# Operands of a seven-product matmul made between plain FFN blocks, with three banks, other groups and longer-lived weight pools

## The chip, the cores and the metric

The kernel runs on one core of one Trainium2 chip. The metric is the device time of one execution in microseconds. A core has a matrix engine (TensorE, PE in the profile, with PEld for its weight loads), VectorE (DVE), ScalarE (ACT), GpSimd (POOL) and SyncE (SP), which here issues nearly all DMAs. On-chip data lies in SBUF; matmuls write to eight PSUM banks.

## What is computed

One step of a one-layer decoder for 512 prompt tokens and 8 x 8 sample tokens, which share all weights: 576 tokens of 1024 channels in float32. Two SwiGLU FFNs enclose a token-mixing part (an RWKV-7 scan, a causal convolution, cross-attention into 256 memory tokens, three gates):

```python
def _swiglu(x, w_up, w_down):
    hg = x @ w_up
    return (jax.nn.silu(hg[..., :D_FF]) * hg[..., D_FF:]) @ w_down

x = x + 0.5 * _swiglu(_rmsnorm(x, p['ffn1_norm']), p['ffn1_w_up'], p['ffn1_w_down'])
m, wkv, shift, conv = _token_mixing(_rmsnorm(x, p['mix_norm']), ...)
x = x + m
x = x + 0.5 * _swiglu(_rmsnorm(x, p['ffn2_norm']), p['ffn2_w_up'], p['ffn2_w_down'])
```

D_FF is 2816. The change is in both FFNs and in the pools that the whole kernel takes its weights from.

## The kernel before

Activations lie with channels on partitions: x is eight tiles of 128 channels x 576 tokens (N), treated as two halves of 288 (H). Precision is kept by splitting each float32 operand into a high and a low part (`split`: ScalarE casts the high part, VectorE subtracts it from the source for the low one), and multiplying three times: high by high, high by low, low by high (`mm3k`, line 94, and line 353).

An FFN (`ffn`) has 22 blocks of 128 hidden channels. A block needs two up-projections (gate and value), a Silu, a product (`hidden`, line 421), and a split into one of the rooms listed in `ROOMS`.

- Blocks 0 to 4 are plain (`plain`): two products of 48 matmuls each over x scaled by the norm weight, then a multiplication by the tokens' 1/rms (line 410). A weight tile of 128 x 1024 is loaded (`wload`, line 70) and split in two halves of 512 columns, each a pair of tiles.
- Blocks 5 to 21 are Strassen blocks (`strassen`): the two up-projections together form a 2 x 2 product of block matrices (gate and value by two token halves, with the 1024 channels in even and odd groups), made from seven products of 12 matmuls, 84 in all where a plain block has 96. Four of the seven weight sides are sums, made by GpSimd (`total`, line 344); four of the token sides are differences. All seven are split. The results are combined by VectorE from three banks (lines 363 to 373).
- The token sides come from `operands`: for each of four pairs of channel tiles, the scaled x and four differences, one of them on GpSimd (line 319), and seven splits. It is written after the five plain blocks and before the first Strassen block. Its scaled x uses the same tiles (t1, t2) as the blocks, its differences the tiles m1 and p.
- Down-projections go by groups of blocks, `FGROUPS` = (4, 4, 4, 4, 2, 4): when a group's hidden tiles are there, its eight down products (`down`, one for each 128 output channels; evicted at line 417) are written behind the blocks of the next group, evenly. The last group's come at the end with the sums of squares of the next norm.

The weight tiles come from two pools, opened anew for each stage: `wp` for raw weights (3 tiles in the FFNs, 2 in the mixing) and `wq` for split pairs (5 and 3). Tile pools hand a buffer on when its last reader is done. The order of instructions on each engine is set when the kernel is built, by a planner that takes the source order as priority, models times, and lets ready work go ahead of work that waits; on the chip each engine's queue and SP's queue run in that order.

At the end of FFN1 the memory tokens are projected to keys and values (`mem_load`, `mem_k`, `mem_v`) around the last norm row, and `mix_norm` makes the mixing stage's operands. The mixing stage's first weights are the `win` tiles; `merge`, between the mixing and FFN2, starts with `wya` weights and four tiles yl (lines 1021 to 1029).

Of the kernel before, what the change touches and what calls it, by code (L numbers as in the profile page):

```python
# [22 lines left out]
FGROUPS = (4, 4, 4, 4, 2, 4)  # L23
PLAIN = 5

ROOMS = (8, 9, 10, 11, 12, 0, 1, 2, 3, 4, 5, 6, 8, 9, 10, 11, 0, 1, 8, 9, 10, 11)
# [23 lines left out]
class _Builder:  # L50
# [16 lines left out]
    def wload(self, src, n, pool=None, tag="", cap=512):  # L67

        w = self.wp.tile([128, 1024], F32, name="w")[:, :n]
        self.dma(w if len(src.shape) == 2 else w.rearrange("p (j c) -> p j c", j=src.shape[1]), src)  # L70
        parts = []
        for c in range(0, n, cap):
            x = w[:, c:min(c + cap, n)]
            hl = [(pool or self.wq).tile([128, cap], F32R, name="w" + t + tag)[:, :x.shape[1]] for t in "hl"]
            self.split(hl[0], hl[1], x)
            parts.append(hl)
        return lambda i, a, b: parts[a // cap][i][:, a % cap:(b - 1) % cap + 1]
# [74 lines left out]
    def build(self):  # L152
        tc, a = self.tc, self.a
        with ExitStack() as st:
            E = st.enter_context
            cp = E(tc.tile_pool(name="cp", bufs=1))
            self.xp = E(tc.tile_pool(name="xp", bufs=1))
# [14 lines left out]
            with ExitStack() as sf:  # L172
                F = sf.enter_context
                self.psum(F, p=8)
                self.wp, self.wq = (F(tc.tile_pool(name=t, bufs=b)) for t, b in (("wp", 3), ("wq", 5)))
# [3 lines left out]
                self.strassen_pools(F)  # L179
                x = [x1p.tile([128, N], F32, name=f"x{k}") for k in range(8)]  # L180
                self.dma(self.pv, a["pv"])
                raw = []
                for n in (2, 2, 2):
                    w = self.wp.tile([128, 1024], F32, name="w")
                    raw += [w[:, 384 * k:384 * (k + 1)] for k in range(n)]
                raw += [self.sp.tile([128, 512], F32, name="p")[:, :384] for _ in range(2)]
# [24 lines left out]
            self.wp, self.wq = (s_ps.enter_context(tc.tile_pool(name=t, bufs=b)) for t, b in (("wp", 2), ("wq", 3)))  # L211
# [36 lines left out]
            self.wp, self.wq = (E(tc.tile_pool(name=t, bufs=b)) for t, b in (("wp", 3), ("wq", 5)))  # L248
# [17 lines left out]
    def strassen_pools(self, F):  # L266

        self.xe = F(self.tc.tile_pool(name="xe", bufs=1))
        self.sp = F(self.tc.tile_pool(name="sp", bufs=3))
# [13 lines left out]
    def rows(self, fp, t, h):  # L283

        r = fp.tile([128, H], F32, name="r" + str(h), bufs=1)
# [12 lines left out]
    def operands(self, x, fp, g, r):  # L298

        V, G = self.V, self.G  # L300
        out = []
        for p in range(4):
            t = []
            for k in (2 * p, 2 * p + 1):
                t.append(fp.tile([128, N], F32, name=f"t{k % 2 + 1}"))
                for h, ri in enumerate(r):
                    c = slice(h * H, (h + 1) * H)
                    V.scalar_tensor_tensor(t[-1][:, c], x[k][:, c], self.par(g, k), ri, ALU.mult, ALU.mult)
            b11, b12, b21, b22 = (u[:, h * H:(h + 1) * H] for u in t for h in range(2))
            t1, t2 = (self.sp.tile([128, 512], F32, name="p")[:, :H] for _ in range(2))  # L310
            t3, t4 = (fp.tile([128, H], F32, name="m1") for _ in range(2))
            ops = {}

            def part(n, src):
                o = ops[n] = self.xe.tile([128, 2, H], F32R, name=n + str(p))
                self.split(o[:, 0], o[:, 1], src)

            part("b11", b11)
            G.tensor_tensor(t3, b12, b22, ALU.subtract)  # L319
            V.tensor_tensor(t1, b11, b12, ALU.subtract)  # L320
            V.tensor_tensor(t2, b22, t1, ALU.add)
            part("t2", t2)
            V.tensor_tensor(t4, b21, t2, ALU.subtract)
            part("b21", b21)
            part("t1", t1)
            part("t4", t4)
            part("b22", b22)
            part("t3", t3)
            out.append(ops)
        return out  # L330

    def strassen(self, fp, wu, i, xs):
# [3 lines left out]
        w = []  # L336
        for m in range(2):
            w.append(self.wp.tile([128, 1024], F32, name="w"))
            self.dma(w[m], wu[i + m])
        a11, a12, a21, a22 = (t.rearrange("p (k e c) -> p k e c", e=2, c=128)[:, :, e, :] for t in w for e in range(2))  # L340
        def total(u, v):
            s = self.sp.tile([128, 512], F32, name="p")
            s = s.rearrange("p (k c) -> p k c", c=128)
            G.tensor_tensor(s, u, v, ALU.add)  # L344
            return s
        def product(p, src, b, first):
            hl = [self.wq.tile([128, 512], F32R, name="w" + t) for t in "hl"]
            v = [t.rearrange("p (k c) -> p k c", c=128) for t in hl]
            self.split(v[0], v[1], src)
            for k in range(4):  # L350
                c = slice(128 * k, 128 * k + 128)
                for q, (l, o) in enumerate(((0, 0), (0, 1), (1, 0))):
                    self.T.matmul(p, hl[l][:, c], xs[k][b][:, o], start=first and k == 0 and q == 0,  # L353
                                  stop=k == 3 and q == 2, skip_group_check=True)
        pa, pb, pc = (self.bank()[:, :H] for _ in range(3))
        m1 = fp.tile([128, H], F32, name="m1")
        t1, t2 = (fp.tile([128, N], F32, name=n) for n in ("t1", "t2"))
        product(pa, a11, "b11", True)
        A.copy(m1, pa)
        p1 = total(a21, a22)  # L360
        p2 = total(p1, a11)
        product(pb, p2, "t2", True)
        V.tensor_tensor(t1[:, H:], pb, m1, ALU.subtract)  # L363
        product(pa, a12, "b21", False)
# [811 lines left out]
```

## Time and profile before

| quantity | value |
|---|---|
| time, median of 3 runs | 1564.11 us (1562.04 to 1569.45) |
| profiled execution, own time | 1566.99 us |
| its span, first to last instruction | 1564.5 us |
| mean granted TensorE clock | 0.962 |
| DMA moved | 144.64 MB, mean 92 GB/s |
| VectorE, ScalarE, GpSimd busy | 64%, 43%, 13% of the span |

The profile shows one execution. Busy time of an engine is the time in which it had at least one instruction under way; overlapping instructions count once. The row of 40 slices gives tenths of each slice of 39 us. The table of stretches gives busy time and counts for chosen windows, and so shows which stage an average hides. The chain of work that ended last is followed back from the end: each piece is a start, a length, and an engine with the tile it wrote.

### The profile page before, as it was taken

How to read it: one execution, taken by the hardware profiler on the slowest of the kernel's cores; microseconds unless marked ns; L12 is line 12 of the kernel's file. 1: busy time of each engine (PE TensorE's matmuls, PEld its weight loads, DVE VectorE, ACT ScalarE, POOL GpSimd, SP SyncE). 2: the span in 40 equal slices, each digit the busy share in tenths (PEclk: the TensorE clock that was granted, in tenths of full speed). 3: DMA queues.
4: the chain of work that ended last, by engine and by line, in shares of the span. 5: the costliest groups of instructions: out<-in, count | busy, mean ns of one | idle time of the engine just before them, and what ended most of it. 6: DMA issues, size and time to landing. Idle time of an engine off the chain costs nothing.

```text
span 1564.5 us, 27277 instructions
## 1 busy us (share of the span) xinstructions
PE 1475.8 (94%) x10786; PEld 1389.8 (89%) x10786; DVE 1000.1 (64%) x1993; ACT 673.3 (43%) x1397; POOL 197.4 (13%) x165
## 2 busy tenths in 40 slices
PE   8959999999989999999999999979996999999987
PEld 8959999998989889878879878769996899999987
DVE  5586676666775559769456455356447666667666
ACT  5343443433456645444446443334333344334342
POOL 0033222222100000000000000000002322231320
PEclk9979999999989999999899999989998899999998
DMA  5212223323543143223213124175211223323222
GB/s 185 75 34 88 82 83 102 100 68 94 157 121 108 42 146 87 58 75 102 64 52 112 42 79 121 53 240 173 93 55 34 81 82 96 108 82 95 78 85 68
DMA packets 97626, 144.64 MB, mean 92 GB/s; under 512 B 43916, under 2 KB 55564, under 8 KB 97500
## 3 DMA queue, kind: packets, MB, share of 16 engines
q1 hardware_dynamic: 96924, 142.33, 29.8%
q8 instruction: 84, 1.38, 0.4%
q10 hardware_dynamic: 576, 0.59, 0.1%
q14 instruction: 42, 0.34, 0.1%
HBM read 126.36 MB, written 16.53 MB: 91 GB/s over the span
## 4 chain that ended last, share of the span: by engine, by line
PE 81%; DVE 10%; DMA 3%; ACT 3%; POOL 2%; issue 1%; SPq 0%; DVEq 0%; POOLq 0%; ACTq 0%
PE p L94 46%; PE p L353 20%; DVE wl L81 2%; PE g L829 1%; DVE t L81 1%; PE c L947 1%; DMA w<-wu 1%; POOL p L344 1%; PE c L951 1%; PE c L944 1%; DVE pr L906 1%; DVE x L417 1%; ACT wh L80 1%; POOL m L319 1%; DMA w<-win 1%
## 5 line engine op out<-in xcount | busy, mean ns | idle before, releaser
L94 PE MATMUL p<-x,wh 128*128 128x288 f32 (+1 forms) x3232 | 679.7, 302 | 13.2 <-ACT wh L80 13.0
L94 PEld LDWEIGHTS p<-x,wh 128*128 128x128 f32 (+1 forms) x3232 | 526.9, 190 | 27.2 <-issue 15.2
L94 PE MATMUL p<-x,wl 128*128 128x288 f32 (+1 forms) x1616 | 485.5, 301 | 1.5 <-DVE wl L81 1.5
L80 ACT CAST wh<-w 128x512 fp32r<-128x512 f32 (+2 forms) x359 | 213.6, 598 | 275.4 <-PE p L94 134.8
L81 DVE TENSOR_TENSOR wl<-w,wh 128x512 fp32r<-128x512 f32 (+2 forms) x359 | 243.1, 679 | 130.8 <-ACT wh L80 121.7
L94 PEld LDWEIGHTS p<-x,wl 128*128 128x128 f32 (+1 forms) x1616 | 306.3, 190 | 7.3 <-issue 3.3
L353 PE MATMUL p<-t,wh 128*128 128x288 f32 x1088 | 224.0, 300 | 19.5 <-ACT wh L80 9.6
L353 PEld LDWEIGHTS p<-t,wh 128*128 128x128 f32 x1088 | 176.2, 191 | 23.9 <-DVE t L363 11.9
L353 PE MATMUL p<-b,wh 128*128 128x288 f32 x816 | 170.6, 301 | 26.2 <-ACT b L80 17.9
L81 DVE TENSOR_TENSOR wl<-p,wh 128x512 fp32r<-128x512 f32 (+1 forms) x138 | 120.0, 874 | 106.5 <-ACT wh L80 105.3
L80 ACT CAST wh<-p 128x512 fp32r<-128x512 f32 (+1 forms) x138 | 82.8, 617 | 193.7 <-POOL p L344 155.9
L353 PE MATMUL p<-t,wl 128*128 128x288 f32 x544 | 161.5, 297 | 0.1
L353 PEld LDWEIGHTS p<-b,wh 128*128 128x128 f32 x816 | 132.7, 191 | 30.1 <-ACT b L80 19.0
L344 POOL TENSOR_TENSOR p<-w 128x512 f32<-128x512 f32 x68 | 88.8, 1306 | 265.7 <-DMA w<-wu 250.8
L353 PE MATMUL p<-b,wl 128*128 128x288 f32 x408 | 121.3, 297 | 0.0
L319 POOL TENSOR_TENSOR m<-t,t 128x288 f32<-128x288 f32 x8 | 13.9, 1731 | 809.1 <-PE p L94 701.0
L344 POOL TENSOR_TENSOR p<-p,w 128x512 f32<-128x512 f32 x68 | 91.7, 1348 | 160.8 <-DVE wl L81 157.4
L353 PEld LDWEIGHTS p<-t,wl 128*128 128x128 f32 x544 | 103.3, 190 | 0.8 <-DVE wl L81 0.8
L353 PEld LDWEIGHTS p<-b,wl 128*128 128x128 f32 x408 | 78.1, 191 | 0.0
L417 DVE SCALAR_TENSOR_TENSOR x<-p,x 128x288 f32<-128x288 f32 x160 | 68.0, 449 | 6.9 <-PE p L94 6.6
L80 ACT CAST x<-t 128x576 fp32r<-128x576 f32 (+1 forms) x60 | 36.4, 610 | 49.4 <-DVE t L421 45.2
L971 DVE SCALAR_TENSOR_TENSOR st<-c,gc,mg 64x64 f32<-64x64 f32 x56 | 15.9, 283 | 58.7 <-PE c L962 58.0
(317 smaller groups left out, 2049.1 us busy)
## 6 DMA issues: line engine op xcount, KB each, us to landing
w<-wu SPq DMA_DIRECT2D x85, 512.0 KB
w<-win SPq DMA_DIRECT2D x44, 512.0 KB
w<-wd SPq DMA_DIRECT2D x80, 256.0 KB
d_mb<-gate SPq DMA_DIRECT2D x16, 288.0 KB
w<-wo SPq DMA_DIRECT2D x8, 512.0 KB
x<-x SPq DMA_DIRECT2D x8, 288.0 KB
d_x<-x SPq DMA_DIRECT2D x16, 144.0 KB
d_g<-gate SPq DMA_DIRECT2D x8, 288.0 KB
```

The lines of the kernel that those rows point to most:

```text
L80: self.A.copy(hi, x)
L81: self.V.tensor_tensor(lo, x, hi.bitcast(F32), ALU.subtract)
L94: self.T.matmul(p, l, x[r][:, c], start=k == 0 and i == 0, stop=k == n - 1 and i == 2)
L319: G.tensor_tensor(t3, b12, b22, ALU.subtract)
L344: G.tensor_tensor(s, u, v, ALU.add)
L353: self.T.matmul(p, hl[l][:, c], xs[k][b][:, o], start=first and k == 0 and q == 0, stop=k == 3 and q == 2, skip_group_check=True)
L417: V.scalar_tensor_tensor(x[m][:, c], p, 0.5, x[m][:, c], ALU.mult, ALU.add)
L829: T.matmul(ps[:, i * 128:(i + 1) * 128], kb[o, c + i].rearrange("p a t -> p (a t)"), ra[o, c + i].rearrange("p a t -> p (a t)"), start=Tru ...
L906: V.tensor_tensor(pr, tt[:, :n, :e].unsqueeze(2).broadcast_to([np_, n, m, e]), l3[:, t:e, :e].unsqueeze(1).broadcast_to([np_, n, m, e]), A ...
L944: T.matmul(ps[64:, 64 * h:64 * h + 64], gr[:64, h, c, 64:], vu[:64, c, 64 * h:64 * h + 64], start=h == 0 or not inter, stop=not inter)
L947: T.matmul(ps[64:, :128], l, r, start=False, stop=i == len(inter) - 1)
L971: V.scalar_tensor_tensor(mn[s, s], ps[s, 256 + 64 * h:320 + 64 * h], gc[s, c:c + 1], mg[s, s], ALU.mult, ALU.add)
```

## The change

In words:

- `operands` makes one set for one pair of channel tiles and is called after plain blocks 1, 2, 3 and 4. The scaled x lies in a tile of its own, n (one buffer), 1/rms in one 576-wide tile rn; differences and splits are done on wide tiles where two lie side by side; all differences are on VectorE.
- `strassen` starts with the product of the sum p2, keeps three banks with two other products between two uses of one, and ends with a22. t2's sign handling changes with the order, the number of VectorE operations doesn't.
- The raw weights of a block are asked for one block ahead (`raws`).
- `FGROUPS` is (6, 4, 4, 4, 4); `ROOMS` follows it.
- Pools wp (2) and wq (3) are opened once for the whole kernel; the FFNs add two raw tiles (we) and one pair (wf), and hand tiles out in turn. So the FFNs have four raw tiles and four pairs, the mixing two and three as before.
- FFN1's first raw weights, the last group's down weights and the memory tokens are split into other tiles of xe. `mem_v` is made in two halves, with the norm row between them.

```diff
-FGROUPS = (4, 4, 4, 4, 2, 4)
+FGROUPS = (6, 4, 4, 4, 4)
+NORMED = 1
-ROOMS = (8, 9, 10, 11, 12, 0, 1, 2, 3, 4, 5, 6, 8, 9, 10, 11, 0, 1, 8, 9, 10, 11)
+ROOMS = (8, 9, 10, 11, 12, 0, 1, 2, 3, 4, 8, 9, 10, 11, 5, 6, 7, 0, 8, 9, 10, 11)
...
+    def weight_pools(self, E=None, raw=0, split=0):
+        self.wps, self.wqs, self.nw, self.nq = [self.wp] * 2, [self.wq] * 3, 0, 0
+        if E:
+            self.wps += [E(self.tc.tile_pool(name="we", bufs=raw))] * raw
+            self.wqs += [E(self.tc.tile_pool(name="wf", bufs=split))] * split
+    def wtile(self):
+        self.nw += 1
+        return self.wps[self.nw % len(self.wps)].tile([128, 1024], F32, name="w")
+    def wparts(self):
+        self.nq += 1
+        return [self.wqs[self.nq % len(self.wqs)].tile([128, 512], F32R, name="w" + t) for t in "hl"]
...
-        self.sp = F(self.tc.tile_pool(name="sp", bufs=3))
+        self.sp = F(self.tc.tile_pool(name="sp", bufs=4))
...
+    def operands(self, x, g, r, p):
+        V = self.V
+        t = self.sp.tile([128, 4, H], F32, name="n", bufs=NORMED)
+        for i in range(2):
+            V.scalar_tensor_tensor(t[:, 2 * i:2 * i + 2].rearrange("p h c -> p (h c)"), x[2 * p + i],
+                                   self.par(g, 2 * p + i), r, ALU.mult, ALU.mult)
+        two = lambda: self.sp.tile([128, N], F32, name="p").rearrange("p (i c) -> p i c", c=H)
+        t13, t24 = two(), two()
...
+        def part(names, src):
+            o = self.xe.tile([128, len(names), 2, H], F32R, name=names[0] + str(p))
+            self.split(o[:, :, 0], o[:, :, 1], src)
...
+        V.tensor_tensor(t13, t[:, 0:2], t[:, 1::2], ALU.subtract)
+        V.tensor_tensor(t24[:, 0], t[:, 3], t13[:, 0], ALU.add)
+        V.tensor_tensor(t24[:, 1], t[:, 2], t24[:, 0], ALU.subtract)
+        part(("t2", "t4"), t24)
+        part(("b11", "b21"), t[:, ::2])
+        part(("t1", "t3"), t13)
+        part(("b22",), t[:, 3:])
...
+    def raws(self, wu, f):
+        w = [self.wtile() for _ in range(2)]
+        for m in range(2):
+            self.dma(w[m], wu[2 * f + m])
+        return w
...
-        product(pa, a11, "b11", True)
-        A.copy(m1, pa)
         p1 = total(a21, a22)
         p2 = total(p1, a11)
         product(pb, p2, "t2", True)
+        product(pa, a11, "b11", True)
+        A.copy(m1, pa)
         V.tensor_tensor(t1[:, H:], pb, m1, ALU.subtract)
+        product(pc, p1, "t1", True)
+        V.tensor_tensor(t2[:, H:], pc, m1, ALU.add)
+        product(pb, total(a11, a21), "t3", False)
+        V.tensor_tensor(t2[:, H:], pb, t2[:, H:], ALU.subtract)
         product(pa, a12, "b21", False)
         A.activation(t1[:, :H], pa, AF.Silu)
...
         product(pc, total(p2, a12), "b22", False)
         V.tensor_tensor(t1[:, H:], pc, t1[:, H:], ALU.subtract)
         A.activation(t1[:, H:], t1[:, H:], AF.Silu)
+        product(pb, a22, "t4", False)
+        V.tensor_tensor(t2[:, :H], pb, m1, ALU.subtract)
...
-        first = [hidden(f, *plain(f)) for f in range(PLAIN)]
-        xs = self.operands(x, fp, g, r)
+        first, xs = [], []
+        for f in range(PLAIN):
+            first.append(hidden(f, *plain(f)))
+            if f and len(xs) < 4:
+                xs.append(self.operands(x, g, rn, len(xs)))
+        nxt = self.raws(wu, PLAIN)
...
+                    w = nxt
+                    nxt = self.raws(wu, f + 1) if f + 1 < NF else None
+                    h.append(hidden(f, *self.strassen(fp, w, xs)))
```

## What was predicted before the run

> **What bounds the kernel now.** I read the page first, then the table of stretches, then the chain that ended last inside the short stretches.
>
> ```profile
> PE 1475.8 (94%) x10786; PEld 1389.8 (89%) x10786; DVE 1000.1 (64%) x1993; ACT 673.3 (43%) x1397; POOL 197.4 (13%) x165
> PE   8959999999989999999999999979996999999987
> ```
> TensorE is busy nearly throughout, so only the slices that dip can be shortened: two deep dips (the third slice and the 31st, one in each FFN) and some shallow ones. The number of matmuls stays the same (17 blocks of 84 and 5 of 96 in each FFN, the same down products), so I count lost matmuls.
>
> ```profile
> 120.00:360.00 240.00, 240.00 (x1803) 239.54 (x1802) 159.03 (x271) 93.52 (x173) 67.79 (x53) 1.00 0.30 89
> 80.00:120.00 40.00, 23.73 (x137) 21.23 (x136) 30.57 (x65) 14.92 (x33) 13.19 (x9) 0.74 0.14 40
> 1180.00:1240.00 60.00, 43.74 (x292) 41.24 (x291) 46.80 (x96) 24.67 (x53) 17.66 (x12) 0.83 0.15 44
> 360.00:420.00 60.00, 53.57 (x391) 51.93 (x390) 44.23 (x83) 26.34 (x56) 14.49 (x11) 1.00 0.32 97
> 1460.00:1520.00 60.00, 53.03 (x390) 51.61 (x389) 39.21 (x70) 22.92 (x47) 16.36 (x12) 1.00 0.26 80
> ```
> The columns are the stretch, its length, busy time and count of PE, PEld, DVE, ACT and POOL, the granted clock and the DMA share. The first row is the dense state: 1803 / 240 = 7.51 matmuls per us, 0.133 us each, at clock 1.00. At that rate the second row should hold 300.5 and holds 137: 21.8 us lost. The third loses 158.7 matmuls (21.1 us), the fourth 59.7 (7.9 us), the fifth 60.7 (8.1 us). The deep dips are the making of the operands:
>
> ```profile
> 81.01 0.67 DVE t L421
> 91.23 1.96 POOL m L319
> 93.22 0.77 ACT t L80 x2
> 94.01 0.46 DVE t L81
> 94.47 0.37 DVE m L323
> 98.20 1.96 POOL m L319
> 107.80 10.94 PE p L353 x66
> 118.73 6.36 PE p L94 x48
> 125.09 11.18 PE p L353 x84
> ```
> In this chain (start, length, work) a set takes 98.20 - 91.23 = 6.97 us; GpSimd's difference, a cast, and then VectorE follow one another, while TensorE has no operand to multiply. The x66 piece at 107.80 ran at 0.166 us a matmul, the x84 piece at 0.133, so 2.2 us of the dip are the low clock after the idle time. The shallow dips are the last four blocks of each FFN, which have only two short down products (24 matmuls) beside them:
>
> ```profile
> 370.59 4.46 DMA w<-wu
> 375.22 1.26 POOL p L344
> 376.55 1.30 POOL p L344
> 377.87 0.63 ACT wh L80
> 378.52 1.12 DVE wl L81
> 392.36 1.26 POOL p L344
> 409.18 3.13 DMA w<-wd
> ```
> One round takes 392.36 - 375.22 = 17.1 us where 108 matmuls take 14.4: a weight buffer comes free late, the load lands 4.5 us after, and two sums on GpSimd follow it.
>
> **The operands.** Removed: the pure operand stage of both FFNs, at most 21.8 + 21.1 = 42.9 us. Added: the same work inside plain blocks 1 to 4. Can VectorE carry it?
>
> ```profile
> 33.00:76.00 43.00, 43.00 (x313) 43.00 (x313) 22.36 (x41) 15.15 (x24) 0.00 (x0) 0.95 0.23 68
> 69.82 0.45 DVE L410 TENSOR_TENSOR t<-p,r 128x288 f32<-128x288 f32 x1
> 70.19 0.94 DVE L308 SCALAR_TENSOR_TENSOR t<-x,pv,r 128x288 f32<-128x288 f32 x2
> 76.00 0.46 DVE L410 TENSOR_TENSOR t<-p,r 128x288 f32<-128x288 f32 x1 [1.90 <-PE p L94]
> 1119.83 0.82 DVE L388 SCALAR_TENSOR_TENSOR x<-x,pv,x 128x576 fp32r<-128x576 f32 x1
> 1120.57 0.75 DVE L296 TENSOR_TENSOR ss<-ss,t 128x576 f32<-128x576 f32 x1
> ```
> A 576-wide scaled product costs 1120.57 - 1119.83 = 0.74 us, a 576-wide difference 0.67 (L421 above), a 288-wide one 0.37 (L323). A new set is two scaled products (1.48), one wide and two narrow differences (0.67 + 0.74), and three wide and one narrow low parts (2.01 + 0.37): 5.27 us on VectorE and none on GpSimd; four sets are 21.1. In the plain blocks VectorE is busy 22.4 of 43.0 us, some 2.4 of it the first set, which the planner had pulled forward (L308 at 70.19 stands ahead of the last L410 at 76.00, so the order on an engine is not that of the source). So 20 + 21.1 = 41.1 of 43.0 us: it fits, with 4% to spare. No TensorE work is left to cover what slips, since the first down group now waits for block 5; before, down products of blocks 0 to 3 could run beside the operands. The remaining hole is at least nothing and at most a whole late set at its old period, 7 us; I take 4 in each FFN, 8 in all, as 4% spare is too little for an in-order queue that also waits for ScalarE's casts. Gain 42.9 - 8 = 34.9.
>
> The clock fell to 0.74 in the dip above. The Trainium skill ("TensorE: Matmul & The Clock Gate", Part 1: The HAM clock gate) says that an idle window of about 3.4 us halves TensorE's clock until it has been busy as long again; the 2.2 us above agree. By that rule my two holes of 4 us would each cost up to 1.7 us more, an estimate from the page's window, and the sum would be some 3 us worse.
>
> **The groups.** (6, 4, 4, 4, 4) gives each of blocks 6 to 21 two down products of 24 or 36 matmuls, so 132 or 156 matmuls a block (17.5 or 20.7 us), more than the 17.1 us of the round above. Only block 5 runs alone. Gain 7.9 + 8.1 = 16.0, less 1.5 per FFN for the last hidden tile and weights, which share slots with the memory tokens in FFN1 (bounds 0 and all 8 per FFN, as the 409.18 wait might stay): 13. The 16 evictions saved per FFN lie beside TensorE and count nothing.
>
> **Product order and weights.**
>
> ```profile
> L81 DVE TENSOR_TENSOR wl<-w,wh x359: 362/691/1770, 6.0 to 1518.1; 128x512 fp32r<-128x512 f32 x161, 128x256 fp32r<-128x256 f32 x16, 128x384 fp32r<-128x384 f32 x3
> ```
> Product 1 now needs both weight tiles and two sums on GpSimd; before, it needed one tile and no sum. A bank now rests two products (3.2 us) between uses, not one. In the dense rows TensorE never waits, so the order itself gains nothing there beyond what the groups already count. Four raw slots replace three, four split pairs five. With four pairs, the last weight (a22, for product 7) is split from the end of product 3 on: 0.63 cast (377.87), 0.46 eviction ahead of it (as L410 above), 0.69 low part (the median in the row above), 0.1 assumed for signals: 1.9 us. Counting the tiles handed out in turn, in FFN1 two successive blocks' weights fall on the same two slots, so the load for the next block can only start then: 1.9 + 4.5 load (4.46 above) + 2.65 for both sums (375.22 to 377.87) + 0.63 + 0.7 = 10.4 us, due after four products and two down products, 6.4 + 6.36 = 12.8: free, by 2.4. In FFN2 the raw tiles rotate by odd counts, the next block's weights are early, and the first down weight takes the late slot: 1.9 + 3.13 + 0.63 + 0.69 = 6.35 us against four products, 6.4. That margin is nothing; I take 0.25 us in each of 16 blocks: loss 4, bounds 0 and 16. On SP these loads queue in the planner's order; a weight load that waits for its slot holds down loads behind it, which is part of the same bound.
>
> **The boundaries.** The raw and split pools now live through the whole kernel, so the next stage's first weights need not wait for the old pools.
>
> ```profile
> 453.85 0.38 ACT kv L499
> 457.04 3.97 DMA w<-win
> 461.11 0.63 ACT wh L80
> 1030.09 0.47 DVE gate L740
> 1033.18 6.10 DMA w<-wya
> 1040.03 97.41 PE p L94 x719
> ```
> ```profile
> 1034.73 0.67 ACT L80 CAST yah<-yl 128x576 fp32r<-128x576 f32 x1 [2.30 <-DMA yl<-d_ya]
> ```
> TensorE stands from 453.85 until 461.11 + 0.63 = 461.74, 7.9 us. With w_in there early and the norm row made between the halves of mem_v, the next operands are eight pairs of 0.47 (L308 above, two in 0.94) + 0.37 on VectorE, 6.7 us, against the second half of mem_v and the first half of the projection, 24 + 24 matmuls (6.4), and then an operand wanted every 0.4 us: about 7 gained (0 to 8). In the merge the gap is 10 us, and once the weight is early the last yl tile is late instead, ready at 1034.73 + 0.67 + 0.67 = 1036.1: 4 gained (0 to 5). Other moves (raw weights split into tiles of their own, ss in another pool) lie beside dense matmuls or the first loads and count nothing.
>
> **Sum.** 34.9 + 13 - 4 + 11 = 54.9 us. The profiled execution took 1566.99 us (span 1564.5 and 2.5 around it), 2.9 above the median of 1564.11: 1512.1 from the one, 1509.2 from the other. I say 1510.
>
> **Rivals.** (a) VectorE becomes the bound in plain blocks: a set and more slips behind block 4 and block 5's splits queue behind it, a hole of 13 us rather than 4 in each FFN: 1510 + 18 = 1528. For it: 96% load; against it: a plain product takes 48 x 0.133 = 6.4 us, and the four pairs hold two of them, so a split may come some 6 us late. (b) Every Strassen block stalls some 0.8 us, from the late slot or slower sums: 33 x 0.8 = 26, 1536.
>
> ```profile
> 77.40 1.09 POOL L319 TENSOR_TENSOR m<-t,t 128x288 f32<-128x288 f32 x1 [76.54 <-DVE t L308]
> 84.22 1.99 POOL L319 TENSOR_TENSOR m<-t,t 128x288 f32<-128x288 f32 x1 [5.73 <-ACT b L80]
> ```
> For (b): the same GpSimd operation took 1.09 or 1.99 us by what VectorE did beside it, and both sums now gate product 1; against it: the margin of 2.4 us in FFN1 covers 0.9 for each. The Trainium skill ("SBUF — State Buffer", Who interferes with whom) has a rule for it: a VectorE instruction with two SBUF inputs and a GpSimd one that reads SBUF exclude each other, and the later blocks; the two durations agree.
>
> (c) The planner puts the operands behind block 4 after all, so the change doesn't do what it says: the 34.9 are not gained, 1545. Against it: it pulled L308 forward at 70.19 as soon as it had a buffer. (d) Slower: the a22 split in FFN1 and FFN2 is served late, behind other work in the ACT and DVE queues. Three products late is 4.8 us against a margin of 2.4 in FFN1 and none in FFN2: 17 x 2.4 + 16 x 4.8 = 118 us, 1628. It decides once blocks stall over 54.9 / 33 = 1.7 us on average; against it, in the dense rows today's splits, served by the same two queues, never make TensorE wait. (e) Several losses of (a) and (b) eat the gain to within 0.5%.
>
> **Chances.** Forecast 0.58, (a) 0.17, (b) 0.10, (c) 0.06, (d) 0.05, (e) 0.04. The range goes from all gains with no hole left (42.9 + 16 + 13 = 72, from the median 1492; 1494) to just over (b), 1540, and leaves out (c) to (e) and some tails. A measurement can tell about 0.5% (8 us) from no change: faster by more 0.91, within 0.04, slower 0.05.
>
> **What would show it.** The two deep dips gone, with a hole under 5 us before the first L353 products and VectorE near full in the plain blocks: the operands. The last four blocks of each FFN at 17.5 us: the groups. TensorE waiting for a down weight at each block of FFN2 but not of FFN1: the slot count. First w_in and wya loads issued before the old stage ends: the boundaries. I am wrong if a hole near 20 us stays after plain block 4, or if Strassen blocks run longer than 17.5 us apiece.

## The result and the profile after

| kernel | median of its runs | ratio to before, 95% interval |
|---|---|---|
| before | 1565.41 us (1562.04 to 1569.45, 4 runs) | 1 |
| changed | 1512.01 us (1508.05 to 1514.89, 4 runs) | 0.9656 (0.9623 to 0.9689) |

The kernel became 53.4 us faster by medians; 1510 was predicted, within 1494 to 1540. One execution of the runs below, 1570.87 us of e12_best_sums, fell into a slower state with a granted clock of 0.838, and the median given for that run is that of its three others. The profiled execution of the changed kernel took 1511.3 us, of which 1509.5 are span: 55.0 less than the 1564.5 of before. The page of the changed kernel gives busy time first and then the 40 slices:

```profile
PE 1471.2 (97%) x10786; PEld 1386.0 (92%) x10786; DVE 1009.4 (67%) x1921; ACT 675.5 (45%) x1373; POOL 194.6 (13%) x157
...
PE   8999999999999999999999999989999999999997
```
The number of matmuls is the same, and the two deep dips (the third and the 31st slice) and the dip of the twelfth slice are gone from the row of slices; that the last blocks are denser only the stretches below show. To see where the 55.0 us come from, I cut both executions at two marks: the copy of the memory values at the end of FFN1, and the first matmul on the yah tiles, with which the merge starts. First before, then changed, from the timeline:

```profile
453.85 0.37 ACT L499 COPY kv<-p 128x256 f32<-128x256 f32 x1 [0.99 <-PE p L94]
...
1040.03 0.61 PE L94 MATMUL p<-yah,wh 128*128 128x288 f32 x1 [10.05 <-ACT wh L80]
```
```profile
431.74 0.36 ACT L526 COPY kv<-p 128x256 f32<-128x256 f32 x1
...
1005.06 1.09 PE L110 MATMUL p<-yah,wh 128*128 128x288 f32 x3 [6.01 <-ACT yah L96]
```

| stage | before | changed | gained | the prediction's terms for it |
|---|---|---|---|---|
| FFN1, to the first mark | 453.85 | 431.74 | 22.1 | 17.4 operands + 6.5 groups = 23.9 |
| mixing, to the second mark | 586.18 | 573.32 | 12.9 | 7 + 4 boundaries = 11 |
| merge and FFN2, to the end | 524.47 | 504.44 | 20.0 | 17.4 + 6.5 - 4 (late slot) = 19.9 |

All three come out within 2 us. The first mark isn't at quite the same place in the work: before, six matmuls of the norm row (0.94 us) run at the mark, and now they run ahead of it, so up to 1 us of FFN1's gain stands in the second row. The stretches show the parts, with the columns as in the prediction:

```profile
33.00:76.00 43.00, 43.00 (x320) 43.00 (x319) 40.88 (x68) 22.25 (x38) 4.71 (x4) 0.98 0.18 62
60.00:120.00 60.00, 56.85 (x410) 55.94 (x410) 48.19 (x72) 24.92 (x45) 17.98 (x12) 0.97 0.22 70
120.00:360.00 240.00, 239.86 (x1783) 237.10 (x1782) 161.34 (x264) 94.77 (x174) 73.67 (x52) 1.00 0.28 87
360.00:400.00 40.00, 39.98 (x299) 39.51 (x298) 29.31 (x57) 19.20 (x39) 5.53 (x4) 1.00 0.48 146
1140.00:1200.00 60.00, 56.52 (x409) 55.62 (x408) 50.04 (x69) 24.08 (x43) 23.28 (x16) 0.97 0.23 73
1200.00:1400.00 200.00, 198.71 (x1481) 196.40 (x1481) 136.62 (x220) 79.08 (x145) 56.00 (x42) 1.00 0.29 90
1400.00:1460.00 60.00, 59.85 (x446) 58.92 (x445) 39.70 (x68) 24.96 (x46) 13.55 (x11) 1.00 0.25 75
```
At the dense rate of before (7.51 matmuls per us) 60 us hold 450.7 matmuls. The second row holds 410, so the dip in FFN1 still loses 5.4 us; the row 1140:1200 holds 409, a loss of 5.5 us. VectorE is busy 40.88 of 43.0 us in the plain blocks. The last blocks run dense: x299 where 40 us at that rate hold 300.5, and x446 of 450.7 in FFN2. But the long rows are no longer quite dense: x1783 where before held 1803, 2.7 us in 240, and x1481 of 1502, 2.8 us in 200. The list of waits says at what TensorE (PE, PEld) then stands, in total, times and longest; the last two rows are of the stretches 100 to 380 and 1180 to 1460 us of the changed kernel, and the single row behind is of 120 to 360 us of before:

```profile
PE p L110 <- ACT yah L96: 6.0, 1, 6.0
PE p L364 <- DVE t L375: 5.8, 8, 1.4
...
PE p L110 <- ACT kv L526: 0.7, 1, 0.7
...
PEld p L364 <- DVE t L375: 3.6, 15, 0.3
...
PEld p L364 <- DVE t L375: 5.2, 15, 0.6
```
```profile
PEld p L353 <- DVE t L363: 0.4, 2, 0.2
```
L375 is the eviction of the sum product t2 from bank pb. It needs m1, the copy (L374) of the product behind it, b11; and t3, two products behind b11 in the source, needs the bank. That wait is in every Strassen block, where the order of before had next to none, and it is also the larger part of the remaining hole. The timeline of TensorE, VectorE, GpSimd and ScalarE there (start, length; idle before in brackets):

```profile
82.97 0.40 PE L364 MATMUL p<-b,wh 128*128 128x288 f32 x1 [0.94 <-ACT m L374]
84.78 0.54 PE L364 MATMUL p<-t,wh 128*128 128x288 f32 x2 [1.41 <-DVE t L375]
...
85.95 0.43 PE L364 MATMUL p<-t,wl 128*128 128x288 f32 x1
...
86.90 0.44 PE L364 MATMUL p<-b,wh 128*128 128x288 f32 x1
87.14 0.44 PE L364 MATMUL p<-b,wl 128*128 128x288 f32 x1
...
89.47 0.43 PE L364 MATMUL p<-b,wh 128*128 128x288 f32 x2
...
79.55 1.85 DVE L435 TENSOR_TENSOR t<-t,t 128x576 f32<-128x576 f32 x1
81.32 1.77 DVE L97 TENSOR_TENSOR wl<-w,wh 128x512 fp32r<-128x512 f32 x1
83.01 0.74 DVE L97 TENSOR_TENSOR x<-t,x 128x576 fp32r<-128x576 f32 x1
83.68 0.68 DVE L97 TENSOR_TENSOR wl<-p,wh 128x512 fp32r<-128x512 f32 x1
84.28 0.44 DVE L375 TENSOR_TENSOR t<-p,m 128x288 f32<-128x288 f32 x1
...
79.16 1.62 POOL L354 TENSOR_TENSOR p<-p,w 128x512 f32<-128x512 f32 x1
80.74 1.80 POOL L354 TENSOR_TENSOR p<-w 128x512 f32<-128x512 f32 x1
...
81.43 0.67 ACT L96 CAST x<-t 128x576 fp32r<-128x576 f32 x1 [2.07 <-DVE t L435]
82.53 0.39 ACT L374 COPY m<-p 128x288 f32<-128x288 f32 x1
```
Block 4's hidden product (L435), the split of its tile and two splits of weights stand in front of L375 on VectorE. Two of them take 1.85 and 1.77 us, with GpSimd's sums (L354) beside them, where the next two, of the same sizes, take 0.74 and 0.68. The copy L374 waits behind the cast of that hidden tile. So TensorE stands for 0.94 us, for the bank of b11, and for 1.41 us, for that of t2, with a single matmul between, and from 85.95 until 89.47 its matmuls start some 0.24 us apart (86.90, 87.14) instead of 0.133.

### The profile page after: what moved, and what is told of

It is laid out like the page before. It is cut to its first block, busy times and chain, and to the rows that moved or that the text cites. A ratio compares the mean times of both kernels' runs of the same rounds, so it can differ in the third digit from the quotient of the medians.

```text
span 1509.5 us, 27178 instructions
## 1 busy us (share of the span) xinstructions
PE 1471.2 (97%) x10786; PEld 1386.0 (92%) x10786; DVE 1009.4 (67%) x1921; ACT 675.5 (45%) x1373; POOL 194.6 (13%) x157
## 4 chain that ended last, share of the span: by engine, by line
PE 87%; DVE 7%; ACT 2%; issue 2%; DMA 1%; SPq 0%; DVEq 0%; ACTq 0%
PE p L110 49%; PE p L364 24%; DVE wl L97 2%; PE g L857 1%; PE c L975 1%; PE c L972 1%; PE c L979 1%; PE g L128 1%; DVE pr L934 1%; ACT wh L96 1%; PE c L1007 1%; PE p L148 1%; PE c L1005 1%; PE c L990 1%; PE c L128 1%
## 5 line engine op out<-in xcount | busy, mean ns | idle before, releaser
L110 PE MATMUL p<-x,wh 128*128 128x288 f32 x3136 | 657.3, 301 | 0.9 <-ACT kv L526 0.7
L110 PEld LDWEIGHTS p<-x,wh 128*128 128x128 f32 x3136 | 508.6, 189 | 14.6 <-issue 7.1
L110 PE MATMUL p<-x,wl 128*128 128x288 f32 x1568 | 470.2, 300 | 1.6 <-DVE wl L97 1.6
L97 DVE TENSOR_TENSOR wl<-w,wh 128x512 fp32r<-128x512 f32 (+1 forms) x353 | 266.5, 759 | 139.8 <-ACT wh L96 132.8
L96 ACT CAST wh<-w 128x512 fp32r<-128x512 f32 (+1 forms) x353 | 209.7, 600 | 259.8 <-PE p L110 120.4
L110 PEld LDWEIGHTS p<-x,wl 128*128 128x128 f32 x1568 | 295.8, 189 | 7.3 <-issue 3.3
L354 POOL TENSOR_TENSOR p<-w 128x512 f32<-128x512 f32 x68 | 94.0, 1382 | 1101.4 <-DVE t L97 759.8
L97 DVE TENSOR_TENSOR wl<-p,wh 128x512 fp32r<-128x512 f32 x136 | 107.8, 792 | 70.8 <-ACT wh L96 69.0
L96 ACT CAST wh<-p 128x512 fp32r<-128x512 f32 x136 | 84.4, 621 | 127.2 <-PE p L110 72.0
L354 POOL TENSOR_TENSOR p<-p,w 128x512 f32<-128x512 f32 x68 | 97.4, 1432 | 65.0 <-DVE wl L97 45.8
L431 DVE SCALAR_TENSOR_TENSOR x<-p,x 128x288 f32<-128x288 f32 x128 | 56.6, 449 | 12.1 <-PE p L110 11.9
L97 DVE TENSOR_TENSOR x<-t,x 128x576 fp32r<-128x576 f32 (+1 forms) x60 | 44.0, 741 | 13.5 <-ACT x L96 13.3
```

What stands on the lines that cost most here:

```text
L96: self.A.copy(hi, x)
L97: self.V.tensor_tensor(lo, x, hi.bitcast(F32), ALU.subtract)
L110: self.T.matmul(p, l, x[r][:, c], start=k == 0 and i == 0, stop=k == n - 1 and i == 2)
L431: V.scalar_tensor_tensor(x[m][:, c], p, 0.5, x[m][:, c], ALU.mult, ALU.add)
```

## The experiments

All are the changed kernel with one edit, unless said otherwise. One finding has to come first, since the comparisons rest on it. The row for the mixing stage between the two marks, of the changed kernel and of e8_sums_on_vector (below), in which the engines have the same order of instructions in that stage, but for one VectorE instruction that moved a few places:

```profile
431.74:1005.06 573.32, 560.24 (x4090) 486.31 (x4091) 352.57 (x805) 281.26 (x658) 4.00 (x15) 0.97 0.30 89
```
```profile
427.35:995.12 567.77, 554.11 (x4091) 481.54 (x4091) 352.48 (x805) 281.08 (x659) 4.00 (x15) 0.98 0.31 90
```
The same work took 573.3 and 567.8 us, at a granted clock of 0.97 and 0.98. The clock that the traces record explains the rest: in this stage TensorE was granted half rate for 38.5 us in the changed kernel and for 26.0 us in e8, and with half of that time taken off, 554.1 and 554.8 us are left. e1 and e9, with 29.0 and 28.0 us at half rate, come to 554.7 and 554.2 in the same way. Why such a spell falls into one execution and not into another isn't shown. The FFN stages have them too, where no edit touches the work: from 20 to 40 us, ahead of the plain blocks, the changed kernel has 137 matmuls at a clock of 0.91, and e1, e5 and e12 have 148 or 149 at 1.00, which is worth 1.5 us. So differences under 2 us in an FFN stage are not told apart. With this in mind I read edits to the FFNs from the two FFN stages of the profiled runs, cut at the same marks, and not from the medians alone:

| run | median, us | ratio to before (95%) | FFN1 | mixing | merge + FFN2 |
|---|---|---|---|---|---|
| changed | 1512.01 | 0.9656 (0.9623 to 0.9689) | 431.74 | 573.32 | 504.44 |
| e1_operands_behind | 1508.15 | 0.9632 (0.9589 to 0.9675) | 430.68 | 569.20 | 505.12 |
| e1b_operands_held | 1562.87 | 0.9991 (0.9968 to 1.0013) | 458.60 | 568.83 | 534.97 |
| e2_shared_tiles | 1514.91 | 0.9678 (0.9647 to 0.9710) | 433.32 | 572.02 | 508.56 |
| e3_light_end | 1527.20 | 0.9772 (0.9741 to 0.9803) | 444.01 | 571.81 | 509.78 |
| e4_b11_first | 1494.86 | 0.9552 (0.9520 to 0.9584) | 424.40 | 571.04 | 500.06 |
| e5_six_plain | 1503.07 | 0.9611 (0.9581 to 0.9641) | 427.96 | 572.63 | 502.21 |
| e6_pools_by_stage | 1513.03 | 0.9676 (0.9637 to 0.9714) | 430.84 | 577.15 | 504.61 |
| e7_not_ahead | 1505.10 | 0.9625 (0.9596 to 0.9653) | 429.33 | 570.35 | 503.42 |
| e8_sums_on_vector | 1496.42 | 0.9569 (0.9533 to 0.9606) | 427.35 | 567.77 | 499.98 |
| e9_yl_on_pool_queue | 1506.83 | 0.9632 (0.9604 to 0.9661) | 430.55 | 568.20 | 504.85 |
| e11_b11_not_ahead_yl | 1489.29 | 0.9518 (0.9492 to 0.9544) | 423.31 | 572.05 | 494.34 |
| e12_best_sums | 1488.99 | 0.9530 (0.9470 to 0.9589) | 421.02 | 572.68 | 492.40 |

**Is it the place of the operands, or the tiles of their own?** e1 puts the calls back behind the plain blocks, in the source:

```diff
-            if f and len(xs) < 4:
-                xs.append(self.operands(x, g, rn, len(xs)))
+        for p in range(4):
+            xs.append(self.operands(x, g, rn, p))
```


> The changed kernel with the four operand sets written after plain block 4 again, in their own tiles. Theory A (own tiles are the cause: the planner fills idle VectorE time whatever the source order): within 6 us of the changed kernel's 1512, hole before the first Strassen products 3 to 8 us per FFN. Theory B (the place in the source is the cause): the sets come after plain block 4, 5.3 us each on VectorE, hole about 20 us per FFN, 1545.

FFN1 and FFN2 took the same as in the changed kernel (-1.1 and +0.7 us; the rest of the medians' 3.9 lies in the mixing stage, which the edit doesn't touch). The stretch of the plain blocks in e1 shows why:

```profile
33.00:76.00 43.00, 43.00 (x326) 43.00 (x326) 42.43 (x72) 22.38 (x39) 5.27 (x4) 1.00 0.19 62
```
VectorE is busy 42.43 us there: the planner pulled the sets forward into the plain blocks by itself. The place in the source alone does nothing. e2 keeps the place and takes the own tile away, with the scaled x in the blocks' tiles t1 and t2 again. As these don't lie side by side, some differences and splits are made in narrower operations, too:

```diff
-        t = self.sp.tile([128, 4, H], F32, name="n", bufs=NORMED)
+        t = [fp.tile([128, N], F32, name=f"t{i + 1}") for i in range(2)]
...
```


> The changed kernel, sets written between plain blocks, but the scaled x in the blocks' own tiles t1 and t2 (two buffers each) and not in a tile n; no difference on GpSimd. Theory A: the sets must take turns with the plain blocks for t1 and t2, so plain blocks are evicted late or sets slip: 6 to 25 us over 1512. Theory B (place in the source is enough): within 4 us of 1512.

It costs 1.6 + 4.1 = 5.7 us in the FFN stages, in the two holes (398 and 385 matmuls from 60 to 120 and from 1140 to 1200 us, for 410 and 409). Either of the two edits leaves nearly all of the gain. No run takes away place and tiles together: the kernel before has neither, but differs in much else. e1b then holds the sets back in earnest, behind the plain blocks in the source and with a copy on ScalarE that needs block 4's hidden tile in front of each scaled product:

```diff
+            self.A.copy(t[:, 2 * i, :1], late[:, :1].bitcast(F32))
...
+            xs.append(self.operands(x, g, rn, p, first[-1][0]))
```


> As the last, but each set also waits for the hidden tile of plain block 4, so it cannot start earlier; tiles and operations as in the changed kernel, plus eight one-column copies. If the overlap with plain blocks is worth what the prediction took (34.9 us), 1512 + 30 to 40 = 1542 to 1552, with VectorE near 50% busy in the plain blocks and a hole of about 20 us per FFN. If most of the gain came from dropping GpSimd's difference and the shared tiles, holes under 12 us each and at most 1530.

```profile
PE p L365 <- ACT wh L96: 26.2, 1, 26.2
```
That wait of the stretch 60 to 140 us is the pure operand stage, longer than that of before, and the whole gain is gone: 26.9 + 30.5 = 57.4 us in the FFN stages. So the overlap is what the change is worth most for.

**What is the remaining hole?** e4 takes away its cause if it is the bank: the product b11 comes first, so that the copy m1 is there before t2's eviction, and t3 comes behind b21:

```diff
+        product(pa, a11, "b11", True)
+        A.copy(m1, pa)
         p1 = total(a21, a22)
         p2 = total(p1, a11)
         product(pb, p2, "t2", True)
-        product(pa, a11, "b11", True)
-        A.copy(m1, pa)
...
+        product(pa, a12, "b21", False)
+        A.activation(t1[:, :H], pa, AF.Silu)
         product(pb, total(a11, a21), "t3", False)
         V.tensor_tensor(t2[:, H:], pb, t2[:, H:], ALU.subtract)
-        product(pa, a12, "b21", False)
-        A.activation(t1[:, :H], pa, AF.Silu)
```


> The seven products in the order b11, t2, t1, b21, t3, b22, t4, so that the bank of t2 rests for two products before t3, and the copy m1 that its eviction needs is made a product earlier. Theory (the waits of the weight loads for that eviction, 3.6 us in FFN1 and 5.2 in FFN2, are the Strassen blocks' remaining loss): these waits under 1 us in all, 4 to 9 us faster than 1512. Rival (they hide another limit, or t4's bank wait takes their place): within 2 us of 1512, with a wait of the same size on the eviction of t3's bank.

```profile
60.00:120.00 60.00, 58.85 (x433) 57.49 (x433) 50.83 (x74) 25.69 (x47) 17.38 (x12) 1.00 0.25 78
120.00:360.00 240.00, 240.00 (x1809) 240.00 (x1808) 175.82 (x270) 97.68 (x177) 78.46 (x54) 1.00 0.29 92
1140.00:1200.00 60.00, 58.47 (x429) 56.88 (x428) 49.15 (x72) 25.64 (x49) 19.47 (x14) 1.00 0.27 84
1200.00:1400.00 200.00, 199.72 (x1507) 199.19 (x1506) 144.25 (x223) 79.61 (x148) 57.87 (x44) 1.00 0.30 90
```
17.1 us faster by medians, more than either theory gave it, 7.3 + 4.4 = 11.7 of them in the FFN stages; the spells at half rate ahead of the blocks are the same as in the changed kernel. In FFN1 the hole lost (450.7 - 410) / 7.51 = 5.4 us and now loses 2.4, and the long row is dense again (1809 for 1783, 3.5 us); in FFN2 the rows gain 20 and 26 matmuls, 2.7 and 3.5 us. The waits for that eviction are gone: of the wait of 3.6 us in the stretch 100 to 380 this row is left:

```profile
PEld p L364 <- issue: 0.4, 1, 0.4
```
The many small waits were the order of the products, and the hole was so for more than half.

e8 asks whether GpSimd's sums make VectorE slow there. The sums of blocks 5 and 6 go to VectorE, so VectorE has more to do:

```diff
-            G.tensor_tensor(s, u, v, ALU.add)
+            (V if early else G).tensor_tensor(s, u, v, ALU.add)
```


> The changed kernel with the eight weight sums of blocks 5 and 6 on VectorE and not on GpSimd. In the changed kernel VectorE's operations between 61 and 83 us took some 6.5 us longer than the same ones elsewhere (1.84 for 0.74, 1.77 for 0.68), whenever GpSimd made such a sum. If GpSimd's sums cause that: VectorE's durations there return to 0.7 to 0.8, it gains about 6 us and pays eight sums of 0.6 (4.8): the hole of FFN1 shrinks by 0 to 2 us and the time is 1507 to 1512. If VectorE's load alone counts and the long durations have another cause: its queue is 4.8 us longer, the holes grow by 3 to 5 us each, 1518 to 1522.

```profile
71.38 0.68 DVE L354 TENSOR_TENSOR p<-w 128x512 f32<-128x512 f32 x1
...
78.20 0.75 DVE L435 TENSOR_TENSOR t<-t,t 128x576 f32<-128x576 f32 x1
...
81.34 0.44 DVE L375 TENSOR_TENSOR t<-p,m 128x288 f32<-128x288 f32 x1
```
```profile
60.00:120.00 60.00, 58.89 (x441) 58.41 (x440) 47.97 (x82) 26.15 (x48) 6.00 (x5) 1.00 0.25 80
120.00:360.00 240.00, 239.83 (x1781) 236.83 (x1780) 161.90 (x265) 95.13 (x174) 73.32 (x52) 1.00 0.29 88
```
L435 takes 0.75 us instead of 1.85, and a sum 0.68 on VectorE instead of 1.6 to 1.8 on GpSimd. The eviction L375 comes at 81.34 instead of 84.28, and the hole loses 1.3 us instead of 5.4. The long row is as before the edit (1781). So the hole took two things, the order and a full VectorE queue, and the small waits the order alone. That is 4.4 + 4.5 = 8.9 us in the FFN stages, again more than expected; the other 5.6 of the profiled difference lie in the mixing stage, where the clock made them. The edit also makes the sums themselves shorter; the run doesn't part that from VectorE's shorter operations, though the lines show the latter in front of the eviction. "SBUF — State Buffer" of the Trainium skill (Who interferes with whom) says that a VectorE instruction with two SBUF inputs and a GpSimd one that reads SBUF contend for a shared read port; the durations 1.85 and 0.75 us agree.

e5 makes block 5 plain as well, so that the operands have a block more:

```diff
-PLAIN = 5
+PLAIN = 6
```


> The changed kernel with six plain blocks: 12 matmuls (1.6 us) more in each FFN, 12.8 us more of plain blocks for VectorE to make operands in, and the first down group ready when block 6 starts. If an overloaded VectorE at the entry to the Strassen blocks makes the hole of 5 us in each FFN: the holes go and 3.2 us are added, 5 to 8 us faster than 1512. If the hole comes from the order of products alone (the bank of t2 waits for its eviction whenever VectorE has a queue): the holes shrink by less than half, 0 to 3 us slower than 1512.

3.8 + 2.2 us less in the FFN stages, although the plain block has 12 matmuls more (1.6 us) in each. Some 1.5 us of each lie ahead of the plain blocks, at a higher clock (148 matmuls for 137 from 20 to 40 us, and in FFN2 206 from 1085 to 1115 us for 195 from 1090 to 1120). But the stretch from 60 to 120 us holds 444 matmuls for 410, a loss of 0.9 us, and the long row stays at 1781. An overloaded VectorE was thus needed for the hole, as e8 says too.

**The groups.** e3 takes (6, 4, 4, 2, 2, 4), which leaves light blocks at the end again, with the raw and down weights each in slots of their own from block 5 on:

```diff
-FGROUPS = (6, 4, 4, 4, 4)
+FGROUPS = (6, 4, 4, 2, 2, 4)
```


> The changed kernel with groups (6, 4, 4, 2, 2, 4), so that the last four blocks of each FFN again have only 24 matmuls of down products beside them, as before the change; and from block 5 on raw Strassen weights stay in two slots and down weights in the two others, in both FFNs (FFN1 of the changed kernel is so already). Theory of the prediction (the light blocks run at the period of load, sums and split, 17.1 us): the gain of 13 to 16 us in 'groups' is given back, 1525 to 1528, and FFN1's last four blocks last 16.5 to 17.5 us each. Rival (new order, four raw slots and three banks would have run light blocks near 14.4 us by themselves): within 5 us of 1512.

```profile
358.61 1.30 POOL p L357
...
375.62 1.30 POOL p L357
```
15.2 us slower, 12.3 in FFN1 and 5.3 in FFN2. In its chain the sums come 375.62 - 358.61 = 17.0 us apart again, the round of 17.1 us of before. The light blocks alone:

```profile
340.00:400.00 60.00, 53.47 (x389) 51.59 (x387) 40.48 (x78) 26.36 (x55) 16.59 (x12) 1.00 0.29 92
```
That is 8.2 us lost, and in FFN2 the stretch from 1420 to 1480 us holds 387, 8.5 us lost. The rest isn't the light blocks. In FFN1 another 6.8 us go behind them, where the loads of the memory tokens and of the last down weights come late (99 matmuls from 400 to 420 us for 150.2). The holes, on the other hand, are 2.1 and 2.5 us smaller (426 and 428 matmuls for 410 and 409), which the slots of their own may have done.

**The weights and the boundaries.** e7 asks a block's raw weights in the block itself, e6 opens the two pools anew for each stage, and e9 gives the yl loads to GpSimd's queue:

```diff
-                    w = nxt
-                    nxt = self.raws(wu, f + 1) if f + 1 < NF else None
+                    w = self.raws(wu, f)
...
```


> The changed kernel with each Strassen block's weights asked for at its own start in the source, not one block ahead. Theory (slots, not the place in the source, decide when a load can start; the planner moves it): within 4 us of 1512. Rival (the place a block ahead is needed, since product 1 now waits for two loads and two sums): at least 0.5 us in each of 33 blocks, 1528 and more, with TensorE waiting for the split of product 1's sum.

2.4 + 1.0 us less in the FFN stages: asking ahead gains nothing, and may cost a little in FFN1, where the stretch of the hole holds 431 matmuls for 410.

```diff
+        self.wp, self.wq = E(self.tc.tile_pool(name="wp", bufs=2)), E(self.tc.tile_pool(name="wq", bufs=3))
         self.wps, self.wqs, self.nw, self.nq = [self.wp] * 2, [self.wq] * 3, 0, 0
...
```


> The changed kernel with the raw and split pools of two and three tiles opened anew for each stage, as before the change; sizes and turns as in the changed kernel. Theory (the longer-lived pools give the 11 us at the two boundaries): 1519 to 1526, with a wait of 6 to 8 us at the first win product and 9 to 11 at the first wya product. Rival (mem_v in halves and the free order did it): under 4 us slower than 1512.

```profile
PE p L111 <- DMA wda<-wda: 8.2, 1, 8.2
PE p L111 <- ACT yah L97: 3.0, 1, 3.0
```
The mixing stage takes 3.8 us more, of which the clock may hold some. At its start TensorE waits 8.2 us for a weight instead of 0.7 us for a copy, 7.5 more. The row names the load that landed last; the product itself reads the split of the first win weight, whose load goes out at 434.81 us. At the merge it waits 3.0 instead of 6.0 us.

```diff
-            self.dma(t, self.d_ya[j])
+            self.G.dma_start(t, self.d_ya[j])
```


> The changed kernel with the four yl loads of the merge issued from GpSimd's queue, which is empty there, and not from SP's, where they stand behind a wo load that waits for a slot and a gate's store. If SP's order holds them back (issued at 1001.29, while three of their sources were stored long before): TensorE's wait of 6.0 us for yah falls to 1 to 3, 3 to 5 us faster than 1512. If their tiles only come free when the mixing's pools end: issued at the same time as before, within 2 us of 1512.

The wait at the merge is 4.9 us instead of 6.0. The mixing stage is 5.1 us shorter, but that is no more than e8 shows without any edit there; only the 1.1 can be put down to the queue. The loads go out 4.8 us ahead of the first product instead of 3.8, and by the profile they had waited for the landing of a wya weight. So SP's order is not what holds them back for the most part; whether it is their tiles isn't shown.

**Together.** e11 has the edits of e4, e7 and e9, and e12 that of e8 besides.

> The three edits that may add up: product order b11, t2, t1, b21, t3, b22, t4; weights asked for in their own block; yl loads on GpSimd's queue. If their effects are separate: 1494.9 less 0 to 7 for the weights and 0 to 5 for yl, 1484 to 1495. If the order already took what the weights' place gave (both shorten the queue ahead of t2's eviction): 1490 to 1496.

> Combines e11 (1489.3 us: product b11 first, raw weights asked in their own block, yl loads from GpSimd's queue) with e8 (the sums of blocks 5 and 6 made on VectorE). Theory A, that the product order and the sums removed the same holes at the first two Strassen blocks: no further gain, 1486 to 1492 us (in e11 the stretch 60 to 120 us already holds 443 matmuls of 450, so at most some 1 us per FFN is left). Theory B, that the part of e8's 16 us which the holes did not explain lies elsewhere and adds up: 1478 to 1483 us.

```profile
60.00:120.00 60.00, 60.00 (x454) 60.00 (x454) 49.58 (x85) 27.16 (x50) 8.36 (x6) 1.00 0.28 86
1140.00:1200.00 60.00, 60.00 (x456) 60.00 (x454) 46.45 (x76) 25.57 (x48) 12.24 (x8) 1.00 0.26 79
```
e11 has a median of 1489.29 us, faster than both kernels. Its FFN stages are 8.4 + 10.1 = 18.5 us shorter than the changed kernel's, where e4 and e7 alone come to 15.1, so their effects add. In e12 (these rows) no hole is left, and its FFN stages are 2.3 + 1.9 us shorter than e11's, but 1488.99 and 1489.29 us don't tell the two apart (theory A's range holds 1488.99). Some 1.5 us of each lie ahead of the plain blocks again (148 matmuls for 137 from 20 to 40 us, 207 for 196 from 1080 to 1110). The product order and the sums thus removed largely the same loss: 11.7 and 8.9 us alone, and the second at most 4.2 on top of e11.

## Why the prediction was right

- **The dips as operand making, TensorE-bound elsewhere: shown.** e1b brings them back (57.4 us) by nothing but the dependency and its eight one-column copies. It loses more than the 34.9 of the operand term, and its wait of 26.2 us is longer than the dips of before. Two reasons are at hand, which no run parts: it holds back all four sets, where before one had been pulled forward, and with a first group of six no down products are there to run beside them, as there were before.
- **VectorE's load in the plain blocks, 41.1 of 43.0 us: measured 40.88.** So close is luck: three operations beside GpSimd's sums (1.49 us at 61.82, 1.84 at 63.83, 1.56 at 72.44) took 2.9 us more than the same ones elsewhere in these blocks (0.75, 0.81, 0.45), which the sum didn't have. The hole, 4 us in each FFN: 5.4 and 5.5. The size of the term held (42.9 - 10.9 = 32.0 gained for 34.9), but the reason given, a late operand set, did not. Product 1 was fed on time: its first matmul follows the last plain block's with no idle time before it,

```profile
77.08 0.42 PE L364 MATMUL p<-t,wh 128*128 128x288 f32 x2
```
  and TensorE stood six us later, for t2's bank, because its eviction queued behind block 4's splits. Rival (a) had the right queue (work slipping behind block 4 on VectorE), with the wrong things late in it and too high a price. The low clock stood in a sentence of its own and not in the sum: half rate for 89.47 - 85.95 = 3.5 us cost about half of that here, inside the 5.4.
- **The groups, 13 us: the light blocks cost 8.2 and 8.5 us in e3,** as the prediction's 7.9 and 8.1 had it; e3's 15.2 us in all hold other terms too. The last blocks of the changed kernel fill x299 of 300.5, so the 1.5 per FFN that was taken off for the last hidden tile was not lost.
- **Product order, 0 in FFN1 and 4 lost in FFN2: the step that failed.** "A bank now rests two products between uses" counted the time from product to product, and not that t2's eviction waits for the copy of the product behind it; the rest that is left is one product. No wait for a down weight shows in FFN2, as the slot count had it; the waits are those for L375, in both FFNs. By e4 the order costs 11.7 us in the FFN stages, a little over half of it in the long rows and the rest in the two holes that the operand term already held; by e8 and e5 the holes go as well when VectorE has less in front of that eviction.
- **Weights a block ahead: hidden, as said;** e7 runs without them and is no slower.
- **The boundaries, 7 + 4.** Before, the list of waits had at the start of the mixing

```profile
PE p L94 <- ACT wh L80: 7.2, 1, 7.2
```
  where now 0.7 us are left, 6.5 less. The first win load goes out well ahead of the mark now, and behind it before (before first, then changed):

```profile
457.04 0.81 SPq L70 DMA_DIRECT2D w<-win  x2
```
```profile
404.66 0.37 SPq L86 DMA_DIRECT2D w<-win  x1
```
  With pools by stage, in e6, it goes out at 434.81, behind that run's mark at 430.84, and the wait is back: this mechanism is shown. At the merge 10.05 became 6.01 us, the 4 predicted; the rest of the 12.9 is within what the stage's clock does. That the pools' lifetime shortened the wait at the merge is refuted: with pools by stage e6 waits only 3.0. Its first wya loads, too, go out at 995.04 us, while the mixing's last products run, where before they went out at 1033.18, behind a gate's store and the yl loads on SP. What put them ahead there was not found.
- **The sum, 54.9 against 55.0 in the spans,** holds in each stage, but its closeness is luck: two wrong steps (a hole from late sets, a late down weight) stood in for one right one, the bank, and some of the mixing stage's gain is its clock. Of the rivals, (b) in small is what happened in the long rows, by a third mechanism; (c) did not happen, and e1 shows that it could not have by source order alone; nothing of (d) shows.

## What to carry to other kernels

Where a planner orders the work, a dependency decides the overlap, and the place in the source need not: look in the trace for what the moved work waits for. When a bank is to be used again, count from the last input of its eviction, and ask what stands in the queue in front of that eviction. Where VectorE is nearly full, moving GpSimd's sums to it can still shorten its queue, if the sums had stretched its own operations.

## What the runs showed of the hardware

- VectorE operations with both inputs in SBUF took 1.85 (576 wide) and 1.77 us (512 wide) beside GpSimd's sums, and 0.75 and 0.68 without them; the sums themselves 1.6 to 1.8 us on GpSimd and 0.68 on VectorE.
- TensorE went to half rate at 85.95 us, after standing for 0.94 and 1.41 us with one matmul between, and stayed there for 3.5 us. In the 3.41 us ahead of that it had been busy for 1.57. The Trainium skill ("TensorE: Matmul & The Clock Gate", Part 1: The HAM clock gate) speaks of an idle window of about 3.4 us; here less sufficed.
- The same instructions of the mixing stage took 567.8 or 573.3 us, with 26.0 or 38.5 us of half rate in them. Why the spells differ was not found; an edit worth under 6 us needs its own stage to be seen, and under 2 us that wasn't enough here.
